# A two-layer encoder trunk on one core: the weight buffers' parts begin at 17 byte offsets, in turn

## The chip, the cores and the metric

The kernel runs on one core of a Trainium2 chip. TensorE multiplies matrices (PE in the profile; its loading of the stationary operand is PEld), VectorE (DVE), ScalarE (ACT) and GpSimd (POOL) do the work on elements, and SyncE (SP) issues the transfers. SBUF is the on-chip memory of 128 partitions; a tile occupies the same bytes of each partition, so that a place in it is a byte address within a partition. The metric is the device time in microseconds (us): 2416.4 us is the median of two runs of the kernel before.

## The reference, cut to what matters

Two layers work on 512 tokens of 1024 features. Each adds four terms to the residual `h`:

```
for i in range(DEPTH):                                   # 2
    h = h + 0.5 * rms_norm(swiglu_ffn(rms_norm(h), up1, down1))
    u = rms_norm(h)
    y = concat(ssd(u @ w_in), mla(u @ w_in), gdn(u @ w_in))
    h = h + rms_norm(y @ w_out)
    h = h + rms_norm(cross_attention(rms_norm(h), rms_norm(mem)))
    h = h + 0.5 * rms_norm(swiglu_ffn(rms_norm(h), up2, down2))
```

The feed-forward blocks have 2816 hidden features; their two matrices, `w_in`, `w_out` and the four matrices of the cross attention, all float32, make up nearly all of the work. Everything is float32 in the reference.

## The kernel before, in words

**Three products for one.** A float32 weight `w` is split into two parts of the type float32r, `whi` (a rounded copy) and `wlo = w - whi`; the normalised input has such parts too, `xhi` and `xlo`. A product is made of three matmuls: hi times hi, hi times lo, lo times hi (`mm3`, `mm3x`).

**Weight units.** The weights come in 487 units of up to 128 partitions x 1024 elements (4096 bytes a partition). `load` fetches a unit into one of four `wraw` buffers. `feed` then makes its parts: ACT copies `wraw` to `whi`, and DVE writes `wraw - whi` to `wlo`. The parts lie in three `whi` and three `wlo` buffers, used in turn. A few units, at the ends of phases, are split into other tiles that are free then (`hid`, `pair`, `xpT`, parts of `xhi` and `xlo`); the change doesn't touch these.

**Who is stationary.** In the projections that the trace names `ch` (the FFN's first matrix, most of `w_in`, the cross attention's queries) a 128 x 128 block of the weights is stationary, loaded by LDWEIGHTS, and the moving operand is `xhi` or `xlo`, 512 columns or, in the first units of a phase, 256 (a half of the tokens). In the projections `dn` (the FFN's second matrix, `w_out`, the cross attention's output) it is the other way round: a block of the activations is stationary (`hid`, `oT`, or `xhi` and `xlo`), and 512 columns of `whi` or `wlo` are moving. `tk` are token-major projections of the mixers, with the weights moving; `kv` are the memory's keys and values. Each matmul has a weight load of its own, and the loads overlap the matmul before them.

**The order.** The computation is written as many streams (generators). While the program is built, a planner (`Weave.run`, with the estimated clock `Clock` and the priorities in `PRIO`) takes the stream that can start first; this fixes the order of instructions on each engine before anything runs. Its costs depend on shapes and types, not on addresses. Engines wait for one another by semaphores.

**Places.** In the built program the tiles that matter here begin at these bytes of a partition; the third column is the remainder by 256:

| tile | begins at | remainder by 256 |
|---|---|---|
| area for dynamic transfers | 0 to 16383 | |
| `xhi`, `xlo` | 39808, 56192 | 128 |
| `whi` (3 buffers) | 88960, 93056, 97152 | 128 |
| `wlo` (3 buffers) | 101248, 105344, 109440 | 128 |
| `hid` (22), `oT` | from 130304 on | 0 |
| `mch`, `xkT`, `xpT`, `xvt`, `xq` | from 133632 on | 0 |
| `mkT`, `mqT`, `E` | from 176928 on | 32 |
| `ident`, `xn` (transposes) | 17024, 121728 | 128 |

Blocks within these tiles begin at multiples of 512 bytes from the tile's start, moving halves of a unit at 0 and 2048. The one exception in the list of large products is `tk`, with units of 272 or 416 columns.

All matmuls and split operations are recorded by one helper, so that the profile shows line 137 for each of them; tiles tell them apart.

Of the kernel before, what the change touches and what calls it, by code (L numbers as in the profile page):

```python
# [10 lines left out]
F32R = mybir.dt.float32r  # L11
# [39 lines left out]
def hf(ap, f):  # L51
    """the heads of parity f"""
    return ap.rearrange("p (j f) n -> p f j n", f=2)[:, f]


def twice(order):
    """there and back; the block at the turn serves both ways"""
    order = list(order)
    return order + order[-2::-1]
# [3 lines left out]
# layer, kind, the gain after it  # L63
# [6 lines left out]
# from the end of an instruction to the start of one that needs it, ns  # L70
# of the streams, and the step from one tile (or column block) to the next; the lower goes first
# [8 lines left out]
# the engine of work that several can do  # L80
# [10 lines left out]
class Clock:  # L91
    """estimated times of the engines and of the instruction streams, for the order of emission"""
# [6 lines left out]
    def dma(self, out):  # L99
        """how long after now a transfer to out ends"""  # L100
        n = 4 * out.shape[0] * free_size(out)
        now = self.stream.t if self.stream else self.t["T"]
        self.queue = max(self.queue, now + 1750.0) + n / 360.0
        return self.queue + 900.0 - now
# [20 lines left out]
class Engine:  # L125
    """an engine whose instructions advance the estimated clock"""
# [52 lines left out]
class Trunk:  # L179
    """what lasts: the residual, the normalised input in two float32r parts, the weights on their way"""  # L180
# [31 lines left out]
    def raw(self, w, k0, nk, *cols):  # L212
        """rows k0*128.. (nk blocks) of w, the columns (c0, n) of each part"""
        if len(cols) == 2 and isinstance(cols[0], int):
            cols = (cols,)
        n = sum(c[1] for c in cols)
        t = self.wp.tile([P, 1024], F32, name="wraw", tag="wraw", bufs=4)
        v = t[:, :nk * n].rearrange("p (k c) -> p k c", k=nk)
        o = 0
        for c0, m in cols:  # L220
            self.nc.sync.dma_start(out=v[:, :, o:o + m], in_=w[k0 * P:(k0 + nk) * P, c0:c0 + m].rearrange("(k p) c -> p k c", p=P))
            o += m
        return v
# [7 lines left out]
    def rstd2(self, ss2, c=1.0):  # L231
        """c / sqrt(ss2[0] + ss2[1] + EPS), the sums divided by c^2"""
        G = self.G
        ss = ss2[:, 0:1]
        G.tensor_scalar(out=ss, in0=ss, scalar1=ss2[:, 1:2], scalar2=EPS / (c * c), op0=ALU.add, op1=ALU.add)
        G.tensor_tensor(out=ss, in0=ss, in1=self.mhalf, op=ALU.pow)
        return ss

    def mm3(self, out, w, k, x, first, last):
        """out += w_k^T x, weights stationary"""  # L240
        mm = self.T.matmul
        mm(out, w[0][:, k], x[0], start=first, stop=False)
        mm(out, w[0][:, k], x[1], start=False, stop=False)
        mm(out, w[1][:, k], x[0], start=False, stop=last)

    def mm3x(self, outs, x, w, k, first, last):
        """outs[q] += x^T w_k[:, q-th part], activations stationary"""
        mm = self.T.matmul
        n = w[0].shape[-1] // len(outs)
        for a, b, f, e in ((0, 0, first, False), (0, 1, False, False), (1, 0, False, last)):  # L250
            for q, o in enumerate(outs):
                mm(o, x[a], w[b][:, k, q * n:(q + 1) * n], start=f, stop=e)


class Weave:
    """The computation as streams of instructions. A stream gives way at each yield: it names the engine that
    it needs next, an event to wait for, or buffers to hold; the one that can start first goes on."""
# [14 lines left out]
    # ---- streams  # L272
    def spawn(self, gen, i=0):
        p, step = PRIO[gen.__name__]
        # at first only the input counts
        s = Stream(gen, p + step * i - 100.0 * (self.event(("x", 0, 1)).t is None and gen.__name__ in ("pre", "half", "square")))
        cur = self.k.clock.stream
        s.t = cur.t if cur is not None else self.base
        if cur is not None:
            s.last = cur.last  # L280
        self.streams.append(s)
        return s.done
# [32 lines left out]
    def run(self, over):  # L315
        """until the event over, or the end of all streams"""
# [29 lines left out]
    # ---- instructions of an engine to choose  # L346
# [18 lines left out]
    # ---- buffers  # L365
# [18 lines left out]
    def bank(self, name, cur=False):  # L384
        """a PSUM bank; cur: one of those kept for projections"""
        ps = self.k.ps.tile([P, S], F32, name=name, tag="ps")
        self.lent[id(ps)] = [cur, ps]
        return ps
# [9 lines left out]
    def release(self):  # L398
        """no projection to come: its banks serve all"""
        self.claim = False  # L400
        self.room["b"] = sorted(self.room["b"] + self.room["cur"])
        self.room["cur"] = []

    def restore(self):
        """banks for the projections of the next phase, those free now first"""
# [8 lines left out]
    # ---- weights  # L414
    def n(self, i):
        """the i-th weight unit of this phase"""
# [15 lines left out]
    def feed(self):  # L432
        """the two float32r parts of each weight unit, ahead of its use"""
        k = self.k
        for i in range(len(self.todo)):
# [3 lines left out]
            if i - NJ in self.first[1:]:  # L439
                # the first units of a phase are there: the last norms before it go first  # L440
# [11 lines left out]
            else:  # L452
                yield {"w": 1}
                hi, lo = (k.wp.tile([P, 1024], F32R, name=q, tag=q, bufs=3) for q in ("whi", "wlo"))
# [17 lines left out]
    def count(self, made, used):  # L472
        """the next split is urgent while less than two units wait for their use"""
# [5 lines left out]
    # ---- the residual  # L479
# [6 lines left out]
    def gains(self):  # L486
        """the gains of this phase's end, when the last ones have served"""
# [7 lines left out]
    def pre(self, t, g, phase, y=None, update=None, xn=None):  # L495
        """x[:, :, t-th 128 columns] = transpose of rms(h[t]) * g; y takes the squares"""
# [59 lines left out]
    def post(self, t, ps, c, gpost, gpre):  # L556
        """h[t] += c * rms(ps) * gpost, then the normalised input of the next phase, or the result"""
# [36 lines left out]
    def scaled(self, t, q, order, ps, g, y, ss2, c, sq):  # L594
        """the sum of squares and the product with the gain, one after the other in a bank"""
# [14 lines left out]
    # ---- projections  # L610
    def chan(self, ps, u, c0, c1, late=False):
        """channel-major: ps[:, c0:c1] = w^T x[:, c0:c1]; late: the lower parts of x come later"""
# [16 lines left out]
    def chans(self, n, nj, sink):  # L629
        """units 0 to n - 1, channel-major; the first nj by token halves"""  # L630
# [22 lines left out]
    def down(self, x, i0, order, c, ready):  # L653
        """h += c * rms(x w) * gain, by token halves; the second takes the blocks in the other order"""
# [49 lines left out]
    # ---- phases  # L704
# [19 lines left out]
    def all(self):  # L724
# [3 lines left out]
        # the gain before each phase  # L728
# [29 lines left out]
    def begin(self):  # L758
        """the first normalised input"""
# [26 lines left out]
    def warm(self, gain, row):  # L786
        """the first gain on all partitions; other products keep the tensor engine's clock up until there is work"""
# [71 lines left out]
    def memory(self):  # L859
        """both layers' normalised memory, transposed, as float32r parts [k, P, 2, NM] in DRAM"""  # L860
# [43 lines left out]
    # ---- memory read  # L904
    def cross(self, l, g):
# [7 lines left out]
        # the heads' output: the second half takes the place of the input  # L913
# [40 lines left out]
    def xsoft(self, h, q, qT, pr):  # L954
        """probabilities of token tiles 2 q and 2 q + 1"""
# [68 lines left out]
    # ---- mixers  # L1024
    def mixer(self, l, g):
# [11 lines left out]
        # the residual waits in DRAM; its tiles hold the gates and (q exp(g_cum))^T meanwhile  # L1037
# [40 lines left out]
    def hold(self):  # L1078
        """the places of the norms between the phases serve the mixers, too"""
# [78 lines left out]
    # ---- constants  # L1158
# [147 lines left out]
    # ---- shared parts  # L1306
# [10 lines left out]
    def seg(self, hl, t, h0, out):  # L1317
        """out[s, 4 heads, l] = exp(sum of da over s < k <= l)"""
# [25 lines left out]
    def mem(self):  # L1344
        """blocks of the normalised memory, at first among the weights on their way, then where q, k, v were"""
# [23 lines left out]
    def kv(self):  # L1369
        """keys (channel-major), half of them at a time, and values (token-major) of the memory, to DRAM"""  # L1370
# [3 lines left out]
        for x in range(3):  # L1374
# [4 lines left out]
            for q in range(KD):  # L1379
# [4 lines left out]
                for j in range(nb):  # L1384
                    yield "T"
                    if x < 2:
                        # the two halves of a bank form one group: its first product alone clears it
# [23 lines left out]
    # ---- gated delta rule  # L1411
# [40 lines left out]
    def gates(self):  # L1452
        """beta, softplus and the decays of the delta rule (4 heads) and of the state space (8 heads)"""
# [13 lines left out]
        # log(1 + z) = 2 atanh(z / (2 + z))  # L1467
# [51 lines left out]
    def gtile(self, t):  # L1519
        """unit vectors, transposes, K K^T and Q K^T of token tile t"""  # L1520
# [44 lines left out]
        # in place: q -> (k beta exp(g_cum))^T, v -> v beta, k -> k exp(g_end - g_cum)  # L1565
# [29 lines left out]
    def solve(self, half):  # L1595
        """inverses of the 16 x 16 diagonal blocks, one system per partition"""
# [27 lines left out]
    def inverse(self, t):  # L1624
        """U = ((I + A)^-1)^T block by block"""
# [56 lines left out]
    def rec(self):  # L1682
        """the states: two heads' on the diagonal of each block"""
# [49 lines left out]
    def gone(self, t):  # L1733
        """q, k, v of tile t have served twice: the place of the first holds w_uq, that of the others the memory"""
# [12 lines left out]
    def gout(self, t, St):  # L1747
# [9 lines left out]
        # one group: its first product alone clears the bank  # L1757
# [30 lines left out]
    # ---- state space  # L1788
# [139 lines left out]
    # ---- latent attention  # L1928
# [40 lines left out]
    def prep(self, t):  # L1969
# [55 lines left out]
        # the scores come with the opposite sign  # L2025
# [90 lines left out]
```

## Time and profile before

| | before |
|---|---|
| median of the runs shown (2415.68 and 2417.12) | 2416.4 us |
| span of the profiled execution | 2413.7 us |
| around the span, to the median | 2.7 us |
| PE busy | 2389.6 us, 99% of the span |
| DVE, ACT, POOL busy | 54%, 41%, 12% |
| TensorE's granted clock | 9 or more tenths of full speed in all 40 slices |

The page gives the span of the profiled execution and no other time of its own; what a run has around its span is taken as the 2.7 us to the median. A matmul's recorded duration runs from its start to its modelled end and overlaps the next one's, so the durations can't be added up. The pace is read from the chain of waits: a piece such as "210.12 PE ch x927" is 927 matmuls that followed each other without a wait in 210.12 us.

### The profile page before, as it was taken

Reading aid. Unit: us, or ns where it says so; the run is one execution under the profiler, and the core shown is the slowest. Engines: PE = TensorE matmul, PEld = TensorE weight load, DVE = VectorE, ACT = ScalarE, POOL = GpSimd, SP = SyncE. Lnnn points to the kernel's source line nnn. Section 1 sums busy time; section 2 is a strip of 40 time slices with the busy share of each in tenths; the row PEclk is TensorE's granted clock in tenths of the full one; section 3 lists DMA queues with packets and bytes.
Section 4 is the critical chain, followed back from the end, with each engine's and each line's share of the span. In section 5 each row is a group of like instructions: output and inputs, shape, how many; then the busy total and the mean of one; then the engine's idle time right before and its main releaser. Section 6 shows DMA issues by size and latency. Waiting matters only on the chain.

```text
span 2413.7 us, 31724 instructions
## 1 busy us (share of the span) xinstructions
PE 2389.6 (99%) x12398; PEld 2010.7 (83%) x12398; DVE 1307.8 (54%) x1926; ACT 985.7 (41%) x1627; POOL 283.7 (12%) x406
## 2 busy tenths in 40 slices
PE   9999999999999999999999999999999999999998
PEld 8888888878889888888888888897788898888887
DVE  5433456887766643334543334578876657333344
ACT  4332344534554542223442223445355545322343
POOL 1000000454200100000000000023442101000000
PEclk9999999999999999999999999999999999999999
DMA  5543455323554333335543334552145644333354
GB/s 175 160 131 96 154 192 142 95 60 120 175 203 168 129 116 96 96 97 183 174 123 96 96 97 174 190 125 84 59 132 176 215 143 140 105 96 96 105 190 151
DMA packets 320972, 323.23 MB, mean 134 GB/s; under 512 B 27075, under 2 KB 262069, under 8 KB 320822
## 3 DMA queue, kind: packets, MB, share of 16 engines
q1 hardware_dynamic: 320822, 321.20, 42.1%
q8 instruction: 97, 1.59, 0.3%
q14 instruction: 53, 0.43, 0.1%
HBM read 301.50 MB, written 19.66 MB: 133 GB/s over the span
## 4 chain that ended last, share of the span: by engine, by line
PE 94%; DVE 4%; ACT 1%; issue 1%; DMA 0%; POOL 0%; SPq 0%; DVEq 0%; POOLq 0%; ACTq 0%
PE ch L137 48%; PE dn L137 27%; PE kv L137 4%; PE tk L137 3%; PE tp L137 1%; PE xs L137 1%; PE xo L137 1%; PE mo L137 1%; PE ms L137 1%; PE iu L137 1%; PE iy L137 1%; PE kk L137 1%; PE mp L137 1%; DVE p L137 1%; DVE pair L137 0%
## 5 line engine op out<-in xcount | busy, mean ns | idle before, releaser
L137 ACT ACTIVATE whi<-wraw 128x1024 fp32r<-128x1024 f32 (+1 forms) x488 | 513.8, 1054 | 994.9 <-PE ch L137 605.0
L137 DVE TENSOR_TENSOR wlo<-wraw,whi 128x1024 fp32r<-128x1024 f32 (+2 forms) x487 | 594.7, 1222 | 594.0 <-ACT whi L137 584.6
L137 PE MATMUL ch<-xhi,whi 128*128 128x512 f32 (+1 forms) x1840 | 676.1, 370 | 0.0
L137 PE MATMUL ch<-xhi,wlo 128*128 128x512 f32 (+1 forms) x1840 | 671.8, 367 | 0.0
L137 PE MATMUL ch<-xlo,whi 128*128 128x512 f32 (+1 forms) x1840 | 659.4, 367 | 0.0
L137 PEld LDWEIGHTS ch<-xhi,whi 128*128 128x128 f32 x1840 | 346.9, 189 | 57.2 <-issue 1.3
L137 PEld LDWEIGHTS ch<-xhi,wlo 128*128 128x128 f32 x1840 | 346.9, 189 | 57.2
L137 PEld LDWEIGHTS ch<-xlo,whi 128*128 128x128 f32 x1840 | 340.4, 189 | 55.8
L137 PE MATMUL dn<-whi,hid 128*128 128x512 f32 x1376 | 381.6, 395 | 0.0
L137 PEld LDWEIGHTS dn<-whi,hid 128*128 128x128 f32 x1376 | 258.2, 188 | 60.0
L137 POOL TENSOR_SCALAR ss<-ss 128x1 f32<-128x1 f32 (+1 forms) x80 | 30.5, 382 | 1673.1 <-ACT jk L137 1527.5
L137 PE MATMUL dn<-wlo,hid 128*128 128x512 f32 x688 | 217.9, 395 | 0.0
L137 DVE TENSOR_TENSOR hh<-sg,ch 128x512 f32<-128x512 f32 x88 | 60.4, 687 | 261.4 <-PE ch L137 257.3
L137 PEld LDWEIGHTS dn<-wlo,hid 128*128 128x128 f32 x688 | 129.5, 188 | 30.5
L137 PE MATMUL tk<-whi,xhi 128*128 128x272 f32 (+2 forms) x192 | 71.5, 372 | 0.0
L137 PE MATMUL tk<-whi,xlo 128*128 128x272 f32 (+2 forms) x192 | 67.4, 351 | 0.0
L137 PE MATMUL tk<-wlo,xhi 128*128 128x272 f32 (+2 forms) x192 | 67.2, 350 | 0.0
L137 POOL TENSOR_TENSOR sr<-tri,hl 128x512 fp32r<-128x512 f32 x48 | 56.4, 1183 | 65.8 <-PE sg L137 40.3
L137 ACT ACTIVATE xhi<-tp 128x512 fp32r<-128x512 f32 x64 | 37.4, 593 | 61.4 <-PE tp L137 60.9
L137 PE MATMUL dn<-whi,xhi 128*128 128x512 f32 x192 | 61.8, 396 | 0.0
L137 DVE TENSOR_TENSOR hid<-hh,hid 128x512 fp32r<-128x512 f32 x88 | 60.2, 685 | 2.4 <-ACT hid L137 2.4
L137 PE MATMUL dn<-wlo,xhi 128*128 128x512 f32 x192 | 60.9, 392 | 0.2
(338 smaller groups left out, 2896.3 us busy)
## 6 DMA issues: line engine op xcount, KB each, us to landing
wraw<-in_ffn_w_up_dram SPq DMA_DIRECT2D x176, 512.0 KB
wraw<-in_ffn_w_down_dram SPq DMA_DIRECT2D x172, 512.0 KB
wraw<-in_w_in_dram SPq DMA_DIRECT2D x32, 512.0 KB
wraw<-in_xa_w_kv_dram SPq DMA_DIRECT2D x32, 512.0 KB
wraw<-in_w_out_dram SPq DMA_DIRECT2D x30, 512.0 KB
wraw<-in_xa_w_o_dram SPq DMA_DIRECT2D x30, 512.0 KB
mch<-memT SPq DMA_DIRECT2D x32, 256.0 KB
xkv<-kvs SPq DMA_DIRECT2D x32, 256.0 KB
```

Of the source, the lines that this page charges most:

```text
L137: return f(*args, **kw)
```

## The change

The two buffers of a unit become 1088 elements wide instead of 1024, and unit number i uses 1024 of them that begin at byte `OFFSETS[i % 17]`: 0, 16, 32, and so on to 240, and 8. `whi` and `wlo` of a unit have the same offset. The six buffers grow by 256 bytes each, and the area for dynamic transfers at the start of SBUF shrinks from 16384 to 8192 bytes; all transfers of this kernel are issued by SP, and none uses that area. All comments are removed as well, and line numbers move by two or three.

```
+OFFSETS = 0, 16, 32, 48, 64, 80, 96, 112, 128, 144, 160, 176, 192, 208, 224, 240, 8
...
             else:
                 yield {"w": 1}
-                hi, lo = (k.wp.tile([P, 1024], F32R, name=q, tag=q, bufs=3) for q in ("whi", "wlo"))
+                o = OFFSETS[i % len(OFFSETS)] // 4
+                hi, lo = (k.wp.tile([P, 1024 + 64], F32R, name=q, tag=q, bufs=3)[:, o:o + 1024] for q in ("whi", "wlo"))
             hi, lo = (q[:, :nk * n].rearrange("p (k c) -> p k c", k=nk) for q in (hi, lo))
...
-    nc = _bacc.Bacc("TRN2", target_bir_lowering=False, num_devices=1)
+    nc = _bacc.Bacc("TRN2", target_bir_lowering=False, num_devices=1, dynamic_dma_scratch_size=8192)
```

The built programs have the same instructions in the same order on all five engines (8671 rows of PE, 1588 of DVE, 1128 of ACT, 355 of POOL, 248 of SP, where a row is a run of equal instructions); only addresses differ. In the changed program `xhi` begins at 31616, the `whi` buffers at 80768, 85120 and 89472, the `wlo` buffers at 93824, 98176 and 102528, and the tiles behind them lie 6656 bytes lower than before. All remainders by 256 in the table above stay what they were, except that a unit's parts now have 128 plus the unit's offset.

## Rows read from the trace of the kernel before

**Rows 1.** The page's first lines: span, and busy time of each engine (instructions)
```profile
span 2413.7 us, 31724 instructions
PE 2389.6 (99%) x12398; PEld 2010.7 (83%) x12398; DVE 1307.8 (54%) x1926; ACT 985.7 (41%) x1627; POOL 283.7 (12%) x406
PEclk9999999999999999999999999999999999999999
```

**Rows 2.** The page's chain that ended last, by engine and tile
```profile
PE 94%; DVE 4%; ACT 1%; issue 1%; DMA 0%; POOL 0%; SPq 0%; DVEq 0%; POOLq 0%; ACTq 0%
```

**Rows 3.** Chain of waits, 1240 to 1530 us: start us, us, engine, line, tile, count
```profile
1239.95 210.12 PE ch L137 x927
...
1455.74 69.71 PE dn L137 x300
```

**Rows 4.** Chain of waits, 795 to 850 us, the cross attention's output
```profile
799.15 5.58 PE dn L137 x24
...
812.55 17.69 PE dn L137 x78
```

**Rows 5.** Instructions by form, PE: form, count | busy us, mean ns | idle before
```profile
L137 PE MATMUL ch<-xhi,whi 128*128 128x512 f32 x1456 | 569.9, 391 | 0.0
L137 PE MATMUL dn<-whi,hid 128*128 128x512 f32 x1376 | 381.6, 395 | 0.0
L137 PE MATMUL dn<-wlo,hid 128*128 128x512 f32 x688 | 217.9, 395 | 0.0
L137 PE MATMUL ch<-xhi,whi 128*128 128x256 f32 x384 | 106.2, 287 | 0.0
L137 PE MATMUL dn<-whi,xhi 128*128 128x512 f32 x192 | 61.8, 396 | 0.0
L137 PE MATMUL kv<-whi,mch 128*128 128x512 f32 x128 | 46.3, 412 | 0.0
L137 PE MATMUL dn<-whi,oT 128*128 128x512 f32 x128 | 38.7, 399 | 0.0
L137 PE MATMUL ch<-xhi,hid 128*128 128x256 f32 x128 | 24.9, 284 | 0.0
```

**Rows 6.** Chain of waits, 428 to 470 us, where other matmuls interrupt the projections
```profile
438.15 5.47 PE ch L137 x24
...
448.83 5.53 PE ch L137 x24
```

**Rows 7.** Instructions by form, PE: matmuls with operands 32 and 0 bytes past multiples of 64
```profile
L137 PE MATMUL ms<-mkT,mqT 96*128 96x128 f32 x160 | 22.8, 281 | 0.0
L137 PE MATMUL tp<-ident,xn 128*128 128x128 f32 x256 | 38.1, 274 | 3.7 <-DVE xn L137 3.7
```

**Rows 8.** Timeline, 1460 to 1466 us, ACT and DVE: start us, us, instruction [idle before <-releaser]
```profile
1461.41 1.06 ACT L137 ACTIVATE whi<-wraw 128x1024 fp32r<-128x1024 f32 x1 [1.73 <-PE dn L137]
1464.15 1.06 ACT L137 ACTIVATE whi<-wraw 128x1024 fp32r<-128x1024 f32 x1 [1.69 <-PE dn L137]
1462.50 1.23 DVE L137 TENSOR_TENSOR wlo<-wraw,whi 128x1024 fp32r<-128x1024 f32 x1 [1.56 <-ACT whi L137]
1465.24 1.23 DVE L137 TENSOR_TENSOR wlo<-wraw,whi 128x1024 fp32r<-128x1024 f32 x1 [1.52 <-ACT whi L137]
```

**Rows 9.** Waits by engine and releaser: us in total, times, longest us
```profile
ACT whi L137 <- PE ch L137: 605.0, 164, 3.9
ACT whi L137 <- PE dn L137: 286.3, 173, 2.1
```

**Rows 10.** Instructions by form, ACT: writes 128 and 32 bytes past a multiple of 256
```profile
L137 ACT ACTIVATE xhi<-tp 128x512 fp32r<-128x512 f32 x64 | 37.4, 593 | 61.4 <-PE tp L137 60.9
L137 ACT ACTIVATE E<-sg 128x512 f32<-128x512 f32 x8 | 4.8, 597 | 2.6 <-PE sg L137 2.6
```

## The prediction

> **What bounds the kernel now.** I read the page's engine line first, then the chain of waits, then the groups by form. PE is busy 99% of 2413.7 us [rows 1], and 94% of the chain that ended last is its own work [rows 2]; the clock was granted in full in all slices [rows 1], the level of 2.4 GHz. So the time is a sum of matmul paces, and a change that moves no instruction can act only through the pace of one matmul or through a late weight unit.
>
> The pace is the surprising view. In a stretch without a wait 927 `ch` matmuls of 512 columns take 210.12 us, 226.7 ns each; 300 `dn` matmuls of the same 512 columns take 69.71 us, 232.4 ns each [rows 3]. 512 columns at 2.4 GHz are 213.3 ns, so the first carry 13.4 ns over the columns and the second 19.1 ns. What differs is not the kind of projection. In the cross attention's output 24 `dn` matmuls take 5.58 us, 232.5 ns each, and a little later 78 of the same projection take 17.69 us, 226.8 ns each [rows 4]; the first have `oT` as stationary operand, the second `xhi` and `xlo`, with the same moving `whi` and `wlo`. By the table of places `oT` and `hid` stand at remainder 0 by 256 bytes, while `xhi`, `xlo`, `whi` and `wlo` stand at 128. In `ch`, and in the fast `dn`, stationary and moving operand have the same remainder; in the slow `dn` they are 128 bytes apart. I take it that the distance of the two operands, as a remainder by 256, sets whether the loads of weights and the streams of columns settle into the pace of 226.7 ns or not (232.4 ns).
>
> A second thing matters: the fast pace must be found again after an interruption. Where other matmuls come in between, 24 `ch` matmuls took 5.47 us and 5.53 us, 227.9 and 230.4 ns each [rows 6], with the same operands that give 226.7 undisturbed.
>
> **The change, part by part.** It adds and removes no instruction. It gives a unit's parts 17 distances in turn. Only the distance 0 (one unit in 17) of `ch`, and the distance 128 for `dn`, are known from rows; fifteen are not. Of an unknown distance I bound the pace by the two that rows show, 226.7 and 232.4, and take their middle, 229.5, because one known distance settles and one doesn't, and because each unit of 24 matmuls now begins with a new distance, as after an interruption. The sum:
>
> - `ch` at 512 columns: 1456 each of three products [rows 5], 4368. They now run at 226.7, and go up by 2.85 ns: +12.4 us. Ends: 0 if all distances settle, 4368 x 5.7 = +25 us if none does.
> - `dn` with `hid` (1376 + 688), `dn` with `oT` (128 + 64), `kv` with moving weights (128 + 64) [rows 5]; of the last two pairs the row with `wlo` isn't shown, it has half as many. These 2448 run at 232.4 and go down by 2.85 ns: -7.0 us. Ends: -14 us, and 0.
> - `dn` with `xhi` and `xlo` stationary: 192 each of three products [rows 5], 576, +1.6 us; ends 0 and +3.3.
> - `ch` at 256 columns: 384 each of three [rows 5], 1152. The mean duration with the distance 128 (`xhi` with `hid`, 284 ns) is 3 ns under that with distance 0 (287 ns) [rows 5]; so a narrow matmul may gain up to 3 ns, -3.5 us, and I take 0. `tk`, whose distances are mixed already, counts 0 too.
> - The offsets that are not multiples of 32 (eight of 16 bytes' kind, and 8), 9 of 17 units, so about 3900 of the 7392 wide matmuls above. No row shows an operand at such a place. The nearest has both operands 32 bytes past a multiple of 64, and its recorded duration is 281 ns, against 274 ns for a transpose of as many columns with both at multiples of 64 [rows 7]; the two are different work, so that little of the 7 ns need be the place. I take 1 ns: +3.9 us. Ends: nothing, and another step of 5.7 ns, +22 us.
>
> Sum 12.4 - 7.0 + 1.6 + 3.9 = +10.9 us. On the span that is 2424.6, and with the 2.7 us around it 2427.3: I say **2427 us**, 0.5% slower.
>
> **What is counted at nothing.** ACT's and DVE's writes to other offsets: a copy to a tile 32 bytes past took 597 ns, one at 128 took 593 [rows 10]. Their cover is wide. In `dn` a unit is split about every 2.75 us: 1.06 us of ACT, 1.23 us of DVE, and both stood idle before it for 1.5 us or more [rows 8], ACT until PE gave a buffer back, in all 605 us in `ch` and 286 us in `dn` [rows 9]. With three buffers, a part that is ready 2.3 us after its buffer came free has one unit more in hand. ACT or DVE would have to take well over twice as long before PE waited. The smaller area at the start of SBUF holds nothing that is used; it only moves tiles by multiples of 512 bytes against each other, and distances of 512 don't matter, since within a unit the blocks step by 512 and `ch` keeps its pace through them [rows 3].
>
> **The rivals.**
>
> *Places don't matter; 2416 us.* The 5.7 ns might come from something else that goes with `hid` and `oT`. For it: the recorded durations differ by only 391 against 395 ns [rows 5]. Against it: [rows 4], where the same projection changes pace with the stationary tile. Here the Trainium skill speaks: SBUF — State Buffer, "Who interferes with whom", gives PE two independent read ports, one for the moving operand and one for the weight load, and says that PE never waits on anyone. By that rule the sum would be 0 and the time 2416.4; the two paces of [rows 3] are not explained by it. Chance 0.2.
>
> *Faster: most distances settle, or settle lower.* 128 would then be an unlucky distance that before stood in all of `dn`. `ch` and the `xhi` part of `dn` stay, `dn` with `hid`, `oT` and `kv` gains 14 us, the narrow ones 3.5: 2399 us. For it: at 256 columns the distance 128 is not the worse one [rows 5]. Against it: the settling itself takes matmuls that run at up to 230.4 ns [rows 6], and now each unit has to settle. Chance 0.15.
>
> *Clearly slower: an operand that begins off a multiple of 32 or 64 bytes needs more reads.* All wide matmuls, moving and stationary, would unsettle (+25 + 3) and the odd offsets would cost a second step (+22) or two (+44): 2467 to 2489 us. It decides once the pace over all distances is more than 6.5 ns over today's 7392 matmuls (48 us). Against it: [rows 7]. Chance 0.12.
>
> *A late unit.* If odd offsets slowed ACT's or DVE's access to more than about 2.5 times, the split would bound `dn`, and each of some 200 units there would cost its excess, 1 us each for one in two: about +100 us. [Rows 10] speak against it. Chance 0.03.
>
> **How the numbers follow.** The forecast of a mix near the middle has chance 0.5, with a range of its own from 2410 to 2445. The range that should hold the time 8 times in 10 takes in the faster rival's 2399 nearly and of the slower one only its lower part: 2400 to 2458. A difference of 2% (48 us), about what a measurement of this kernel can tell from no change, would need the upper half of the slower rival or the late unit: 0.09. Faster by 2% would need 6.5 ns off all wide matmuls, a pace no stretch here shows: 0.02.
>
> **What would show it.** In the changed kernel's chain of waits the long pieces of `ch` should have about 228 to 231 ns a matmul instead of 226.7, and those of `dn` with `hid` 229 to 232 instead of 232.4, with the pace changing from unit to unit; ACT's and DVE's mean for the split should stay at 1.06 and 1.23 us, with as much idle time before them, and PE's busy share at 99%. If `ch` keeps 226.7 everywhere, the distance doesn't matter and my reading is wrong; if a pace over 236 ns shows at odd offsets, alignment has a price of its own; if PE waits for `whi` or `wlo`, the split is what failed.

## The result, and the profile after

The changed kernel takes 2435.5 us (2435.16 and 2435.89) against 2416.4: a ratio of 1.008, with a 95% interval from 1.0061 to 1.0099. It is slower by 19.1 us; 2427 was forecast. The span grew by 20.5 us, from 2413.7 to 2434.2.

The page's first lines, to be held against [rows 1], and the chain's shares, against [rows 2]:

```profile
span 2434.2 us, 31724 instructions
PE 2408.4 (99%) x12398; PEld 2007.4 (82%) x12398; DVE 1306.8 (54%) x1926; ACT 987.2 (41%) x1627; POOL 285.0 (12%) x406
PEclk9999999999999999999999999999999999999999
...
PE 93%; DVE 4%; ACT 1%; POOL 1%; issue 1%; DMA 0%; SPq 0%; DVEq 0%; POOLq 0%; ACTq 0%
```

PE's busy time grew by 18.8 us, nearly all of the difference; DVE and ACT stayed within 1.5 us, and the granted clock in its top tenth. PE's idle time within the span grew by only 1.7 us (24.1 to 25.8), so it did not begin to wait: it does the same 12398 matmuls more slowly. The chain of waits shows where. First the kernel before, 1260 to 1440 us and then 1480 to 1516 us (start us, us, what, count), where nothing interrupts either projection:

```profile
1259.89 180.20 PE ch L137 x795
...
1479.91 36.26 PE dn L137 x156
```

The same stretches of the kernel after:

```profile
1259.83 180.28 PE ch L139 x778
...
1479.83 36.31 PE dn L139 x156
```

`ch` went from 226.7 ns a matmul to 231.7, `dn` with `hid` from 232.4 to 232.8. The long stretch of `ch` hides what happens in it: the pace now changes from unit to unit. The chain of the kernel after, cut to one unit at a time, for the offsets 0, 16, 32, 96, 192 and 8 in this order:

```profile
1342.69 5.45 PE ch L139 x24
...
1348.37 5.21 PE ch L139 x23
...
1353.82 5.36 PE ch L139 x23
...
1376.16 5.38 PE ch L139 x23
...
1409.69 5.26 PE ch L139 x23
...
1431.84 5.31 PE ch L139 x23
```

227, 227, 233, 234, 229 and 231 ns a matmul. A piece of 24 or 23 matmuls is short, so the same was read from all starts in the trace: the time from one start to the next, where the matmuls before and after are of the same kind, in `ch` the next has the same offset, and the time is under 300 ns. The distance is the start of the moving operand minus that of the stationary one, as a remainder by 256 (in `ch` it is minus the offset, in `dn` with `hid` and `oT` 128 plus the offset; an offset of 8 is 248 and 136).

| distance | `ch`, 512 columns | `dn` with `hid`, `oT` |
|---|---|---|
| 0 | 226.9 | 229.4 |
| 16 | 228.0 | 231.4 |
| 32 | 233.4 | 233.6 |
| 48 | 233.2 | 232.4 |
| 64 | 229.0 | 230.4 |
| 80 | 229.8 | 230.6 |
| 96 | 233.3 | 234.0 |
| 112 | 233.4 | 230.8 |
| 128 | 233.3 | 232.0 |
| 144 | 233.3 | 233.0 |
| 160 | 233.8 | 233.9 |
| 176 | 231.8 | 234.0 |
| 192 | 233.2 | 232.5 |
| 208 | 233.3 | 234.1 |
| 224 | 233.0 | 232.9 |
| 240 | 227.0 | 228.0 |
| 248 (`ch`), 136 (`dn`) | 230.8 | 235.8 |

Mean ns from start to start in the changed kernel, 225 to 266 matmuls each in `ch`, 106 to 164 in `dn`. In `ch` 0 and 240 (which is -16) give the fast pace, 16 nearly; ten of the 17 lie at 233 to 234. The two columns agree in their best places, 0 and 240, and in that 64 and 80 are better than most others, although the weights are stationary in one and moving in the other. At 16 they disagree (228.0 and 231.4).

A mean over a unit hides that the pace can change within it. Two units of the kernel after, each cut in its chain into the first matmuls and the others: `ch` at the distance 16, which comes after a unit at 32, and `dn` at the distance 0, which comes after one at 240 (its first matmul left out).

```profile
1331.69 1.16 PE ch L139 x5
...
1332.85 4.31 PE ch L139 x19
```

```profile
1157.68 1.62 PE dn L139 x7
...
1159.30 3.63 PE dn L139 x16
```

`ch` begins at 232 ns a matmul and goes on at 226.8, `dn` begins at 231 and goes on at 226.9. Over eight such units of `ch` the first four matmuls took 231.7 ns from start to start and the others 226.7; over ten of `dn` the first eight took 231.4 and the others 226.6. So the pace can need some matmuls to settle behind a new distance, and 16 in `ch` and 0 in `dn` do settle.

The split operations were not touched by their odd offsets. ACT's and DVE's groups by form in the kernel after (count | busy us, mean ns | idle before, with what ended it):

```profile
L139 ACT ACTIVATE whi<-wraw 128x1024 fp32r<-128x1024 f32 x474 | 502.0, 1060 | 981.7 <-PE ch L139 630.0 <-PE dn L139 289.3 <-PE kv L139 25.1
L139 DVE TENSOR_TENSOR wlo<-wraw,whi 128x1024 fp32r<-128x1024 f32 x473 | 580.6, 1228 | 596.9 <-ACT whi L139 582.7 <-DMA b_gdn_dt_bias<-in_gdn_dt_bias_dram 5.2 <-DMA wraw<-in_w_out_dram 0.2
```

1060 ns and 1228 ns against 1.06 and 1.23 us [rows 8], and ACT waits a little longer for PE than before (630.0 and 289.3 us against the 605.0 and 286.3 of [rows 9]).

### The profile page after: what moved, and what is told of

It is laid out like the page before. It is cut to its first block, busy times and chain, and to the rows that moved or that the text cites. A ratio compares the mean times of both kernels' runs of the same rounds, so it can differ in the third digit from the quotient of the medians.

```text
span 2434.2 us, 31724 instructions
## 1 busy us (share of the span) xinstructions
PE 2408.4 (99%) x12398; PEld 2007.4 (82%) x12398; DVE 1306.8 (54%) x1926; ACT 987.2 (41%) x1627; POOL 285.0 (12%) x406
## 4 chain that ended last, share of the span: by engine, by line
PE 93%; DVE 4%; ACT 1%; POOL 1%; issue 1%; DMA 0%; SPq 0%; DVEq 0%; POOLq 0%; ACTq 0%
PE ch L139 49%; PE dn L139 27%; PE kv L139 3%; PE tk L139 3%; PE tp L139 1%; PE xs L139 1%; PE xo L139 1%; PE mo L139 1%; PE ms L139 1%; PE iy L139 1%; PE iu L139 1%; PE kk L139 1%; PE mp L139 1%; DVE pair L139 1%; DVE p L139 0%
```

## The experiments

All start from the changed kernel. The kernel before had a median of 2416.1 us beside the first four and 2416.3 us beside the last three; the ratios are against it.

**All offsets 0.** Is it the offsets, or the wider buffers and the smaller area?

```
-OFFSETS = 0, 16, 32, 48, 64, 80, 96, 112, 128, 144, 160, 176, 192, 208, 224, 240, 8
+OFFSETS = 0,
```

> All 17 offsets are 0; the wider buffers and the smaller area at the start of SBUF stay. Distance theory (a wide matmul's pace hangs on moving start minus stationary start, as a remainder by 256; 0 and -16 give 226.7 ns, most others 230 to 234): ch back at 226.7 ns a matmul, dn with hid at 232.4, 2416 us. Rival, that the buffers' spacing (4352 instead of 4096 bytes) or the move of all tiles costs: 2430 us or more, ch over 228 ns.

2416.9 us, ratio 1.0001 [0.9992, 1.0010]. `ch` (1260 to 1440 us) and `dn` (1480 to 1516 us) in the chain of this kernel:

```profile
1259.87 180.20 PE ch L139 x795
...
1479.84 36.25 PE dn L139 x156
```

Both are back at 226.7 and 232.4 ns. So the whole loss belongs to the offsets; the 256 bytes between the buffers, the moved tiles and the halved area are free.

This kernel also shows that the distance counts as a remainder by 256 and not by 512. The prediction took every move of tiles against each other for a multiple of 512 bytes. In fact the wider buffers leave three of the six an odd multiple of 256 bytes from `xhi` (85120 - 31616 is 209 x 256). Over the whole run `ch` at 512 columns took 227.0 ns from start to start on these buffers (1927 matmuls) and on the other three (2385).

**A constant offset of 32.** Does the distance cost, or that it differs from unit to unit?

```
+OFFSETS = 32,
```

> Every unit's offset is 32, so no unit begins with another distance than the one before. Distance theory: ch at 233 ns (4368 x 6.3 ns = +27 us), dn with xhi at 233 (+3), dn with hid at 234 (+3): 2449 us, slower than the change itself. Resettling theory (the change costs because the distance differs from unit to unit, and any constant one settles): ch within 1 ns of 226.7, 2416 to 2420 us. Alignment theory (an operand that begins off a multiple of 64 or 128 bytes costs): as the distance theory, about 2449.

2447.4 us, ratio 1.013 [1.0114, 1.0145]: 31 us slower than before, and 12 us slower than the change itself. The same two stretches:

```profile
1259.79 180.37 PE ch L139 x773
...
1479.83 36.32 PE dn L139 x155
```

233.3 and 234.3 ns: a distance that doesn't settle doesn't settle in 773 matmuls either. The theory that only the turn of the distances costs is out.

**Everything 32 bytes later.** The offsets are 0 again, and a tile of 32 bytes ahead of the residual moves both operands.

```
         self.mhalf = c.tile([P, 1], F32, name="mhalf")
+        c.tile([P, 8], F32, name="pad")
```

> Offsets all 0, but 32 unused bytes lie ahead of the residual, so that xhi, xlo, whi, wlo, hid, oT and all tiles behind them begin 32 bytes later and all their distances stay as in the kernel before. Distance theory: ch 226.7 ns, dn with hid 232.4, 2416 us. Alignment theory: as with the constant offset 32 or worse, since now both operands begin off a multiple of 64 bytes: ch 233 ns or more, 2449 us or more.

2416.5 us, ratio 1.0000 [0.9991, 1.0009]:

```profile
1259.91 180.20 PE ch L139 x795
...
1479.88 36.25 PE dn L139 x156
```

226.7 and 232.4 ns, with both operands 32 bytes past a multiple of 128. Weights that begin 32 bytes later cost 6.6 ns a matmul if `xhi` stays, and nothing if it moves along. It is the distance of the two operands, not the place of either, as far as a common move by 32 bytes can tell.

**The activations at the weights' remainder.** Offsets 0, and 128 unused bytes behind the weight buffers, so that `hid`, `oT`, `mch`, `xkT`, `xpT`, `xvt` and `xq` come to the remainder 128.

```
         self.mhalf = c.tile([P, 1], F32, name="mhalf")
+        self.tmp.tile([P, 32], F32, name="pad", tag="pad")
```

> Offsets all 0, and 128 unused bytes lie behind the weight buffers and ahead of hid, oT, mch, xkT and the others, which so come to the remainder of the weights and of xhi. Distance theory: dn with hid, oT and kv fall from 232.4 to 226.7 to 227.5 ns (2448 x 5 to 5.7 ns), ch stays at 226.7: 2402 to 2405 us, faster than both kernels. If the slower dn has another reason (the phases' own traffic, or hid itself): dn stays at 232.4 and the time at 2416.

2404.9 us, ratio 0.9950 [0.9937, 0.9962]: faster than both kernels, by 11 and by 31 us. The two stretches, and the cross attention's output (795 to 850 us), whose pieces answer to [rows 4]:

```profile
1259.88 180.20 PE ch L139 x795
...
1479.98 36.04 PE dn L139 x159
```

```profile
795.70 5.47 PE dn L139 x24
...
808.86 17.68 PE dn L139 x78
```

`dn` with `hid` runs at 226.7 ns (36.04 us for 159). In the cross attention the piece of 24 with `oT` went from 232.5 to 227.9 ns, the one of 78 with `xhi` and `xlo` stayed (226.8 and 226.7). The slower pace of `dn` with `hid` and `oT` before was that of its distance, and 128 bytes of padding took it away.

**0 and 16 in turn.** What does the turn cost by itself, between two distances that both settle?

```
+OFFSETS = 0, 16
```

> Offsets 0 and 16 in turn: two distances that both settle at 227 ns in ch in the changed kernel, but another one at each unit. If the turn of distances costs nothing by itself: ch 227 ns, 2417 to 2419 us (half of the dn with hid at distance 144, 233.0 instead of 232.4). If each unit has to settle anew, the first 8 or so of its 24 matmuls at 230 to 231 ns: ch 228 to 228.5, 2422 to 2425 us.

2418.3 us, ratio 1.0006 [0.9998, 1.0015]; no difference that can be told. The chain, 1260 to 1440 us:

```profile
1259.89 180.20 PE ch L139 x795
```

226.7 ns, as with one distance. The second expectation (228 to 228.5 ns, 2422 us or more) is refuted for `ch`: a new distance each 24 matmuls is nearly free between these two. In `dn` it isn't. With `xhi` and `xlo` it has the distances 0 and 16 in turn in this kernel, and after a unit at 16 the first eight matmuls at 0 took 230.3 ns from start to start, the others 226.7 (15 units); in the changed kernel the same was seen above at 0 after 240. Other work in between costs something too: in the kernel before, the first four 512-column `ch` matmuls behind another kind of matmul took 231 to 233 ns, those from the 13th on 226.5 to 226.8.

**A constant offset of 8.** Does an address off a multiple of 16 have a price of its own?

```
+OFFSETS = 8,
```

> Every unit's offset is 8, the one that is no multiple of 16. From the paces of that one unit in 17 in the changed kernel: ch 230.8 ns (+3.8 x 4368 = +17 us), dn with hid 235.8 (+3.3 x 2448 = +8), dn with xhi 232.8 (+3): 2444 us. If an address off a 16-byte line had a price of its own on top of the distance, ch would be the slowest of all offsets, over 234 ns, and the time over 2455 us.

2434.1 us, ratio 1.0075 [1.0060, 1.0091], 10 us under the first expectation, and no sign of the second. The two stretches, and before them a run of 42 `ch` at 256 columns (724 to 744 us):

```profile
730.74 4.86 PE ch L139 x42
...
1259.95 180.15 PE ch L139 x781
...
1479.95 36.17 PE dn L139 x155
```

`ch` came as foretold, 230.7 ns, which is less than at 32. The sum missed in two terms. `dn` with `hid` ran at 233.4 ns instead of 235.8: in the mixture the first eight matmuls of such a unit took 237.1 ns and the others 233.3, so that its mean held the price of the turn too. And the 256-column `ch`, left out of the expectation, gained: 115.9 ns from start to start against 119.8 with distance 0, 1152 x 3.9 = 4.5 us. With these, 4368 x 3.7 + 2448 x 1.0 + 576 x 5 - 4.5 = +17 us; measured were 17.8.

**Narrow units 64 bytes later.** On top of the kernel with padded activations.

```
-                o = OFFSETS[i % len(OFFSETS)] // 4
+                o = 16 if any(0 <= i - f < NJ for f in self.first) else 0
```

> As with hid and the rest at the weights' remainder and all offsets 0, but the first four units of each phase, which the 256-column ch matmuls use, begin 64 bytes later (distance -64). In the changed kernel the one unit in 17 with that distance ran 44 such matmuls at 113.6 ns, against 119.8 at distance 0. If the distance is what sets it: 1152 x 6 ns = -7 us against the kernel with all offsets 0, 2397 to 2399 us. If that was chance or belonged to the place of this unit: 2404 to 2405 us.

2400.4 us, ratio 0.9933 [0.9920, 0.9945], the fastest of all: 16 us under the kernel before. The wide matmuls keep their pace. The narrow ones show in a short stretch, a run of 42 (724 to 744 us), first in the kernel before:

```profile
727.36 5.03 PE ch L137 x42
```

and in this one:

```profile
725.99 4.95 PE ch L139 x42
...
1259.87 180.20 PE ch L139 x795
...
1479.97 36.04 PE dn L139 x159
```

Over the whole run the 256-column matmuls took 116.1 ns from start to start instead of 119.9: 1152 x 3.8 = 4.4 us, and 4.4 were gained against the 2404.9 us with padded activations alone. The 113.6 ns of the one unit in the changed kernel were not reached, so the expected 6 ns were too many.

## Why the prediction was right, and which terms were mis-sized

The direction and the step were right: the distance of moving and stationary operand, as a remainder by 256, sets the pace of wide matmuls, and no other part of the kernel moved by more than 2 us. What it named as its evidence, the two paces in one projection [rows 4], held up when the distance alone was changed (233.3 ns at offset 32, 226.7 ns for `dn` after 128 bytes of padding). The sum was 10.9 us; the span grew by 20.5. By its terms, each from the sum of all times from start to start in the two traces:

| term | forecast | measured |
|---|---|---|
| `ch`, 4368 matmuls | +12.4 | +19.4 (995.0 to 1014.4 us) |
| `dn` with `hid`, `oT`, and `kv`, 2448 | -7.0 | about -1 (`hid`: 481.2 to 480.3) |
| `dn` with `xhi`, `xlo`, 576 | +1.6 | +2.4 (133.1 to 135.5) |
| `ch` at 256 columns, 1152 | 0 | -1.0 (142.5 to 141.5) |
| offsets off a multiple of 32 | +3.9 | 0 |

- **The middle, 229.5 ns, was the step that failed in size.** It came from "one known distance settles and one doesn't". In `ch` three of 17 distances settle (0, 240, and 16 after its first matmuls), two come to 229 to 230 ns and two to 231 to 232; the other ten lie at 233 to 234, above the 232.4 that the prediction took for the upper bound. The mean over the stretch from 1260 to 1440 us is 231.7 ns in `ch`, and `dn` has 232.8: both a little over what the prediction said would show it (up to 231 and 232). For the same reason `dn` gained next to nothing: its distance 128 was as bad as most others, not unlucky among good ones.
- **The resettling is real, but not what makes it slow.** The prediction used it as a second reason for the middle. Constant 32 is slower than the mixture (233.3 against 231.7 ns in `ch`), and 0 and 16 in turn keep 226.7 ns in `ch`. But the first matmuls behind a new distance can run slower, four in `ch` at 16 and eight in `dn` at 0; and a unit in `dn` mostly serves 12 matmuls at a time, not 24, as its 2.75 us [rows 8] at 232.4 ns say. For a single distance that is little: 2.7 ns (229.4 against 226.7) on a 17th of 2448 matmuls is 0.4 us, an estimate from the table and the padded kernel.
- **Places off a multiple of 32 have no price of their own.** In `ch` the eight odd multiples of 16 average 231.2 ns, the eight multiples of 32 232.0; 8 has 230.7. The 1 ns taken from [rows 7] compared two different kinds of work. The terms of `ch` and of `dn` with `hid` were 13 us too low together; the 3.9 us of this term, which measured 0, made up a part of that by luck.
- **What was counted at nothing was nothing:** ACT and DVE, the wider buffers, the smaller area (ratio 1.0001 with all offsets 0).
- **The rival that places don't matter** fell with the result: 6.6 ns a matmul came and went with 32 bytes between PE's own two operands, while both could move together (32 bytes later: 226.7 ns). The Trainium skill, SBUF — State Buffer, "Who interferes with whom", gives PE two independent read ports and says that PE never waits on anyone. By that rule the distance of the two operands would not count, and in these runs it does. Whether the two reads wait for each other is not shown.

Not settled is why 256, and why 16 settles in `ch` (226.7 ns after the first four matmuls) and not in `dn` (231.4). The traces give starts of matmuls and of weight loads, not what the two reads wait for; no experiment here changed what could tell it.

## What to carry to other kernels

When PE is busy all the time, compare the pace of equal matmuls, n of them in a piece of the chain of waits, between projections: if two paces differ, look at the start addresses of moving and stationary operand before anything else. For this shape (float32r, 128 x 128 weights, 512 columns) allocate both with the same remainder by 256 bytes; 128 bytes of padding gave 0.5% here, and cost no time. The narrow matmuls here were faster at another distance than the wide ones, so measure each width.

## What the runs showed of the hardware that was not expected

- A wide float32r matmul with its own weight load takes 226.7 ns at the distance 0, whichever of the two operands the weights are, and 228 to 236 ns at most others (means of the mixture, and of constant offsets). With the weights stationary -16 and, after four matmuls, 16 come to 226.7 as well.
- The pace can need some matmuls to settle behind other work or a new distance: four in `ch` at the distance 16 (231.7 ns, then 226.7), eight in `dn` at the distance 0 (231.4, then 226.6).
- At 256 columns the distance 0 is not the best: 119.8 ns there, 115.9 at -8, 116.1 at -64.
- A common shift of both operands by 32 bytes changes nothing (ratio 1.0000), and offsets of 8 and of odd multiples of 16 cost ACT's and DVE's 1024-element passes nothing (1060 and 1228 ns).
